# A two-layer diffusion backbone in f32 on one core: the last feed-forward with rstd behind the first product and the second product by token rows

## The chip, the cores and the metric

One core of a Trainium2 chip runs the whole program in one launch. The metric is the device time of one execution in microseconds, as the median of several runs; smaller is better. All inputs, weights and the output are float32 in device memory.

## The reference

A stream `x` of 256 latent tokens and a stream of 256 context tokens, both of width D = 1024, go through two layers. Each layer is a feed-forward, a token mixer and another feed-forward. Layer 0 mixes by latent attention, layer 1 by windowed attention. The last feed-forward and the final norm exist for the latent stream alone. What matters here, cut to the second feed-forward of the last layer and the end:

```python
def rms_norm(x, g):
    return x * lax.rsqrt(jnp.mean(x * x, axis=-1, keepdims=True) + EPS) * g

h = rms_norm(x, norm_g[layer, 2]) * (1.0 + mx[7]) + mx[6]     # modulate
g, u = jnp.split(h @ w_in, 2, axis=-1)                         # w_in 1024 x 5632
x = x + 0.5 * mx[8] * ((jax.nn.silu(g) * u) @ w_out)           # w_out 2816 x 1024
return rms_norm(x, final_norm_g)
```

`mx[c]` are nine vectors of 1,024 (shift, scale, gate for three sub-layers) from silu(c) @ mod_w + mod_b.

## The kernel before, in words

**Layout and products.** Features lie on the partitions: `xs[d]` holds features 128 d to 128 d + 127 of all tokens, latent ones in columns 0 to 255 (`X`), context ones in columns 256 to 511. A product runs in three f32r matmuls per block of 128 input features (`mm3`, lines 205 to 212): high half by high half, high by low, low by high. Activations and weights are split into such halves by `split` (lines 179 to 186): a cast on ACT makes the high half, a subtraction on DVE the low half. A matmul has a weight block of 128 x 128 as its stationary operand and tokens as columns: 512 where both streams go through, 256 for the latent stream alone.

**Weights** come as tiles of 512 KB through SP's DMA queue into a ring of three raw buffers and are split into rings of four high and four low buffers (`weight`, lines 188 to 203). PSUM has eight banks, all from one ring (`bank`, line 45).

**Sub-layers.** `Sublayer` (lines 249 to 338) prepares the normalized input of the next feed-forward or mixer while the sub-layer before ends. `closing` (lines 360 to 398) computes the last product of a sub-layer by output tiles of 128 features: `residual` (line 357, DVE) adds each to `xs[d]`, `grown` squares it (line 236, ACT) and sums the squares on POOL (line 242). Then `load_table` (line 247) loads ACT's table for the square root, `prefetch` loads the first two weights, and `stream` (line 279) makes rstd (`rstd_of`: column sums of the squares by a matmul with `ones`, line 221; root, line 223; reciprocal, line 225), scales every x by gain and rstd (lines 287, 288, 290) and splits it (lines 182, 183, 185, 186). Only then can `leading` (line 310) run the first two tiles of the next product.

**The last feed-forward** (`ffn`, lines 403 to 424, called on the last line of the program's body with `Final` as its follower): for each of 22 tiles of 128 of d_ff a gate and an up product of 24 matmuls each, SiLU (line 416), multiplication (line 418) and split. The tiles come in three groups of 8, 7 and 7; after each group `closing` multiplies the group by `w_out` and adds all 1,024 output features to `xs`. `Final` (lines 340 to 352) then makes rstd once more, scales, and writes eight transfers of 128 KB, features on partitions; the host transposes.

**Modulation vectors in the background.** `mod_in_background` (lines 142 to 161) computes one of the nine vectors by eight loads of 512 KB and eight accumulations on DVE (lines 149, 151), a sum over partitions on PE (line 157) and transposes (line 102). `pump` (line 169) issues a piece at a time between other work. The gate of the last feed-forward, vector 8 of layer 1, is made in the feed-forward ahead of the windowed attention.

**Order.** Every engine works its queue in order. A scheduler of the framework fixes that order when the program is built, from program order and a model of when each instruction is ready; `behind` (line 163) ties one instruction behind another by hand.

Of the kernel before, what the change touches and what calls it, by code (L numbers as in the profile page):

```python
# [10 lines left out]
F32 = mybir.dt.float32  # L11
# [3 lines left out]
ALU = mybir.AluOpType  # L15
# [22 lines left out]
def hybrid_backbone_kernel(ctx, tc, t, out):  # L38
# [298 lines left out]
                    mm3(o[:M, :w], self.terms(wt, M, slice(0, w)))  # L337
                    yield o

    class Final(Sublayer):  # L340


        def stream(self, s):
            r = self.rstd(s)
            for k in range(KT):
                y = strip()
                if k in POOL:
                    nc.gpsimd.tensor_tensor(y, xs[k][:, SL[s]], r, ALU.mult)
                    nc.scalar.activation(y, y, AF.Copy, scale=fng[:, k:k + 1])
                else:  # L350
                    nc.vector.scalar_tensor_tensor(y, xs[k][:, SL[s]], fng[:, k:k + 1], r, ALU.mult, ALU.mult)
                nc.sync.dma_start(out[k], y)

    def residual(l, chunk, d, o, streams):
        for s in streams:
            c = chunk * KT + d
# [46 lines left out]
    def ffn(sl, nxt, per_tile=0):  # L403
        l, which, streams = sl.l, sl.sub // 2, sl.streams
        w = T * len(streams)
        outs = sl.products(ffn_specs(l, which))
        done = sl.end
        for g, (f0, f1) in enumerate(GROUPS):
            gu = []
            for f in range(f0, f1):  # L410
                pump(per_tile // 2, done)
                og = next(outs)
                pump(per_tile - per_tile // 2, done)
                ou = next(outs)
                sg = tmp()
                nc.scalar.activation(sg[:, :w], og[:, :w], AF.Silu)  # L416
                pr = tmp()
                nc.vector.tensor_tensor(pr[:, :w], ou[:, :w], sg[:, :w], ALU.mult)  # L418
                hl = (r2k(), r2k())
                done = split(hl[0][:, :w], hl[1][:, :w], pr[:, :w])  # L420
                gu.append(hl)
            last = g == len(GROUPS) - 1
            closing([(t[f"wout{g}"][l, which, d], gu) for d in range(KT)], 2 + 6 * which, l, streams,
                    nxt if last else None, 2 if last else 0, per_tile // 2)


# [377 lines left out]
        closing([(t["swo"][d], O) for d in range(KT)], 5, l, (0,), nxt, 0)  # L804


    def load_tmp(name, n):
        s = r2k(n).bitcast(F32)
        nc.sync.dma_start(s, t[name])
        return s  # L810
# [47 lines left out]
    for k in range(1, KT + 1):  # L858
# [4 lines left out]
            inputs(k)  # L863
        if k in (1, 3, 5):
            lead_weight(sl.hi)
    fng = load_const("fng", (P, KT))
    qng = load_const("qng", (P, 4))
    kvng = load_const("kvng", (P, 2))
    ropeC = load_const("ropeC", (P, T))
# [24 lines left out]
    sl, nxt = nxt, Sublayer(1, 0, (0, 1), ffn_specs(1, 0)[:4])  # L894
    ffn(sl, nxt, 2)
    pump(1000)
    background.extend(mod_in_background(1, c, (0,)) for c in range(5, 9))
    sl, nxt = nxt, Sublayer(1, 1, (0, 1), [(t["swq"][m], 1024) for m in range(2)], (0,))
    ffn(sl, nxt, 2)
    pump(1000)  # L900
    sl, nxt = nxt, Sublayer(1, 2, (0,), ffn_specs(1, 1)[:2])
    swa(sl, nxt)
    ffn(nxt, Final(1, 3, (0,), ()))

def _layout(x, c, ctx, c_ctx, mod_w, mod_b, norm_g, final_norm_g, ffn_w_in, ffn_w_out, mla_w_down, mla_q_norm,
            mla_kv_norm, mla_w_uq, mla_w_ukv, mla_w_o, swa_w_qkv, swa_sink, swa_w_o, **unused):
    a = {}

    def put(name, v):
        a[name] = np.ascontiguousarray(v)

    def cols(v, n):
        return v.reshape(v.shape[:-1] + (n, P))

    def tiles(w, m):

        k, n = w.shape
        return w.reshape(k // P, P, n // m, m).transpose(2, 1, 0, 3)  # L920

    put("xT", np.concatenate([x[0].T, ctx[0].T], axis=1).reshape(KT, P, TT))
    put("cond", np.stack([c[0], c_ctx], axis=-1).reshape(KT, P, 2).transpose(1, 0, 2))
    put("modb", cols(mod_b, 72).transpose(2, 0, 1))
    put("ng", cols(norm_g, KT).transpose(3, 0, 1, 2))
    put("fng", cols(final_norm_g, KT).T)
    put("qng", cols(mla_q_norm[0], 4).T)
    put("kvng", cols(mla_kv_norm[0], 2).T)
    put("modo", mod_w[0][:, :2048].reshape(2, 4, P, 2, KT, P).transpose(4, 3, 0, 2, 1, 5).reshape(KT, 2, 2, P, 512))
    put("modw", mod_w.reshape(2, KT, P, 9, 1024).transpose(0, 3, 1, 2, 4))  # L930
    put("win", ffn_w_in.reshape(2, 2, KT, P, 2, NF, P).transpose(0, 1, 5, 4, 3, 2, 6).reshape(2, 2, NF, 2, P, 1024))
    wo = ffn_w_out.reshape(2, 2, NF, P, KT, P)
    for g, (f0, f1) in enumerate(GROUPS):
        put(f"wout{g}", wo[:, :, f0:f1].transpose(0, 1, 4, 3, 2, 5).reshape(2, 2, KT, P, (f1 - f0) * P))
    put("wdown", tiles(mla_w_down[0][:, :768], P).reshape(6, P, 1024))
    put("wkr", tiles(mla_w_down[0][:, 768:], 64).reshape(P, 512))
    uq = mla_w_uq[0].reshape(4, P, MLA_H, 192)
    put("wqn", uq[..., :128].reshape(4, P, 4, 2, P).transpose(2, 1, 3, 0, 4).reshape(4, P, 1024))
    put("wqr", uq[..., 128:].reshape(4, P, 2, 2, P).transpose(2, 1, 3, 0, 4).reshape(2, P, 1024))
    ukv = mla_w_ukv[0].reshape(2, P, MLA_H, 256)  # L940
    put("wkn", ukv[..., :128].reshape(2, P, 2, 4, P).transpose(2, 1, 3, 0, 4).reshape(2, P, 1024))
    put("wv", ukv[..., 128:].reshape(2, P, 2, 512).transpose(2, 1, 0, 3).reshape(2, P, 1024))
    put("mwo", tiles(mla_w_o[0], P).reshape(KT, P, 1024))
    put("swq", tiles(swa_w_qkv[0][:, :1024], P).reshape(8, P, 1024))
    put("swk", tiles(swa_w_qkv[0][:, 1024:1280], P).reshape(2, P, 1024))
    put("swv", swa_w_qkv[0][:, 1280:].reshape(2, 4, P, 256).transpose(0, 2, 1, 3).reshape(2, P, 1024))
    put("swo", tiles(swa_w_o[0], P).reshape(KT, P, 1024))
    put("sink", np.broadcast_to(swa_sink[0][None, :], (P, 16)))

    pos = np.arange(T)  # L950
    inv = np.exp(np.float32(-math.log(10000.0)) * np.arange(16, dtype=np.float32) / np.float32(16)).astype(np.float32)
    ang = np.concatenate([(pos // 64).astype(np.float32)[:, None] * inv, (pos % 64).astype(np.float32)[:, None] * inv], axis=-1)
    cos, sin = np.cos(ang).T.astype(np.float32), np.sin(ang).T.astype(np.float32)
    put("ropeC", np.concatenate([cos, cos, cos, cos]))
    put("ropeS", np.concatenate([-sin, sin, -sin, sin]))
    swap = np.zeros((P, 3, P), np.float32)
    row = np.arange(P)
    swap[row, 0, row ^ 32] = 1.0
    for half in range(2):
        swap[row, 1 + half, row % 64 ^ 32 | 64 * half] = 1.0  # L960
    put("perm", swap.reshape(P, 3 * P))
    put("ident", np.eye(P, dtype=np.float32))
    i, j = np.arange(P)[:, None], np.arange(P)[None, :]
    far = np.stack([np.where(j > i, NEG, 0.0), np.where(j < i, NEG, 0.0)], axis=1)
    put("band", far.astype(np.float32).reshape(P, 2 * P))
    return a
# [16 lines left out]
```

## Time and profile before

| | |
|---|---|
| median of 3 runs | 1747.94 us (1747.8 to 1748.0) |
| the profiled execution | 1748.32 us, of it 1746.3 us span from first to last instruction |
| PE / DVE / ACT / POOL busy | 1688.0 / 1088.4 / 669.7 / 187.6 us |
| mean granted TensorE clock | 0.989 of full speed |
| read from device memory | 240.11 MB, 138 GB/s over the span |

Times in the rows below are microseconds from the start of the span. A matmul's recorded time is longer than its slot, since matmuls overlap: the distance between two starts tells what one costs. PEld is the weight load, which runs beside the matmul before it.

### The profile page before, as it was taken

The numbers are of one execution on the slowest core, as the hardware profiler recorded it, in microseconds if no ns is written. First come the engines' busy times: TensorE is split into PE (matmuls) and PEld (weight loads), VectorE is DVE, ScalarE is ACT, GpSimd is POOL, SyncE is SP. The second block draws the span as 40 slices with busy tenths as digits, with TensorE's granted clock in tenths as the row PEclk, the third lists the DMA queues.
The fourth block names the chain that finished last, engine by engine and source line by source line (L and its number), as shares of the span: only waits on it lengthen the run. The fifth ranks groups of instructions, "written<-read, shape, count | busy, mean of one in ns | idle before, by whom it ended". The sixth has DMA issues, their size and how long they took to land.

```text
span 1746.3 us, 23850 instructions
## 1 busy us (share of the span) xinstructions
PE 1688.0 (97%) x9428; PEld 1439.0 (82%) x9428; DVE 1088.4 (62%) x1592; ACT 669.7 (38%) x1121; POOL 187.6 (11%) x183
## 2 busy tenths in 40 slices
PE   7999999999999999999999999999999989989997
PEld 4688888888788898888888888888888888889997
DVE  4877576646767467856946474645433679755554
ACT  4422222234556353222222342222222577554443
POOL 1000000004132130000000220000000452110001
PEclk9999999999999999999999999999999999999999
DMA  9556355431212126644735245634322221145552
GB/s 339 173 199 192 129 192 180 157 121 55 85 49 73 49 84 201 206 145 156 219 126 170 93 143 183 216 114 158 103 97 86 89 84 51 55 145 181 173 191 96
DMA packets 72831, 242.71 MB, mean 139 GB/s; under 512 B 8848, under 2 KB 10640, under 8 KB 72720
## 3 DMA queue, kind: packets, MB, share of 16 engines
q1 hardware_dynamic: 72720, 241.20, 41.9%
q8 instruction: 74, 1.21, 0.3%
q14 instruction: 37, 0.30, 0.1%
HBM read 240.11 MB, written 1.05 MB: 138 GB/s over the span
## 4 chain that ended last, share of the span: by engine, by line
PE 55%; DVE 4%; ACT 2%; issue 1%; POOL 1%; DMA 0%; POOLq 0%; ACTq 0%; DVEq 0%
PE bank L210 18%; PE bank L211 18%; PE bank L212 18%; DVE small L444 1%; DVE r2k L183 1%; PE bank L157 1%; DVE wlo L183 0%; DVE strip L225 0%; POOL r2k L183 0%; ACT r2k L182 0%; POOL r2k L287 0%; DVE small L457 0%; PE bank L102 0%; ACT whi L182 0%; DVE x L464 0%
## 5 line engine op out<-in xcount | busy, mean ns | idle before, releaser
L210 PE MATMUL bank<-r2k,whi 128*128 128x512 f32 (+1 forms) x2610 | 918.4, 353 | 9.3 <-ACT r2k L185 4.7
L211 PE MATMUL bank<-r2k,whi 128*128 128x512 f32 (+1 forms) x2610 | 915.3, 351 | 9.8 <-POOL r2k L183 6.1
L212 PE MATMUL bank<-r2k,wlo 128*128 128x512 f32 (+1 forms) x2610 | 912.2, 350 | 4.1 <-POOL wlo L183 2.2
L182 ACT CAST whi<-wraw 128x1024 fp32r<-128x1024 f32 (+1 forms) x313 | 321.7, 1028 | 886.8 <-PE bank L211 527.8
L210 PEld LDWEIGHTS bank<-r2k,whi 128*128 128x128 f32 x2610 | 494.6, 190 | 89.9 <-ACT whi L182 9.2
L211 PEld LDWEIGHTS bank<-r2k,whi 128*128 128x128 f32 x2610 | 496.2, 190 | 78.8 <-POOL r2k L183 8.6
L212 PEld LDWEIGHTS bank<-r2k,wlo 128*128 128x128 f32 x2610 | 495.7, 190 | 69.4 <-POOL wlo L183 3.0
L183 DVE TENSOR_TENSOR wlo<-wraw,whi 128x1024 fp32r<-128x1024 f32 (+1 forms) x302 | 362.9, 1204 | 134.7 <-ACT whi L182 124.7
L151 DVE SCALAR_TENSOR_TENSOR big<-modraw,conds,big 128x1024 f32<-128x1024 f32 x196 | 242.2, 1279 | 13.9 <-DMA modraw<-in_modw 13.3
L357 DVE SCALAR_TENSOR_TENSOR x<-bank,mod,x 128x256 f32<-128x256 f32 x192 | 85.7, 478 | 179.9 <-PE bank L212 179.9
L242 POOL TENSOR_TENSOR strip<-strip 128x256 f32<-128x256 f32 x64 | 65.2, 1032 | 1137.1 <-ACT strip L236 1110.4
L418 DVE TENSOR_TENSOR tmp<-bank,tmp 128x512 f32<-128x512 f32 (+1 forms) x88 | 54.9, 624 | 179.6 <-PE bank L212 177.7
L183 DVE TENSOR_TENSOR r2k<-bank,r2k 128x512 fp32r<-128x512 f32 (+2 forms) x107 | 62.0, 616 | 18.2 <-ACT r2k L182 17.9
L182 ACT CAST r2k<-bank 128x512 fp32r<-128x512 f32 (+2 forms) x107 | 52.4, 541 | 16.4 <-PE bank L212 15.7
L183 DVE TENSOR_TENSOR r2k<-tmp,r2k 128x512 fp32r<-128x512 f32 (+1 forms) x88 | 54.4, 618 | 1.5 <-ACT r2k L182 1.4
L182 ACT CAST r2k<-tmp 128x512 fp32r<-128x512 f32 (+1 forms) x88 | 49.7, 566 | 9.9 <-DVE tmp L418 9.5
L416 ACT ACTIVATE tmp<-bank 128x512 f32<-128x512 f32 (+1 forms) x88 | 47.3, 538 | 6.8 <-PE bank L212 6.8
L444 DVE TENSOR_REDUCE small<-bank 128x1 f32<-128x512 f32 (+1 forms) x64 | 37.7, 614 | 0.3 <-PE bank L645 0.2
L236 ACT ACTIVATE strip<-x 128x256 f32<-128x256 f32 x80 | 30.5, 410 | 17.9 <-DVE x L357 17.0
L225 DVE RECIPROCAL strip<-strip 128x256 f32<-128x256 f32 x14 | 24.5, 1750 | 19.9 <-ACT strip L223 19.9
L186 DVE SCALAR_TENSOR_TENSOR r2k<-r2k,mod 128x256 fp32r<-128x256 f32 x45 | 30.3, 696 | 8.7 <-ACT r2k L185 8.5
L450 ACT ACTIVATE tmp<-bank,small 128x512 f32<-128x512 f32 x32 | 21.9, 688 | 18.4 <-DVE small L446 12.3
(152 smaller groups left out, 1067.1 us busy)
## 6 DMA issues: line engine op xcount, KB each, us to landing
wraw<-in_win SPq DMA_DIRECT2D x172, 512.0 KB, 3.5
modraw<-in_modw SPq DMA_DIRECT2D x128, 512.0 KB, 4.2
wraw<-in_wout SPq DMA_DIRECT2D x64, 448.0 KB, 3.3
wraw<-in_wout SPq DMA_DIRECT2D x32, 512.0 KB, 3.5
r2k<-in_modo SPq DMA_DIRECT2D x32, 256.0 KB, 5.7
wraw<-in_mwo SPq DMA_DIRECT2D x8, 512.0 KB, 3.5
wraw<-in_swq SPq DMA_DIRECT2D x8, 512.0 KB, 3.5
wraw<-in_swo SPq DMA_DIRECT2D x8, 512.0 KB, 3.4
```

The source lines that it names most:

```text
L151: nc.vector.scalar_tensor_tensor(acc[s], raw, conds[:, kt, s:s + 1], acc[s], ALU.mult, ALU.add)
L182: nc.scalar.copy(hi, src)
L183: return engine.tensor_tensor(lo, src, hi.bitcast(F32), ALU.subtract)
L210: nc.tensor.matmul(o, lhsT=ah, rhs=bh, start=(i == 0), stop=False)
L211: nc.tensor.matmul(o, lhsT=ah, rhs=bl, start=False, stop=False)
L212: nc.tensor.matmul(o, lhsT=al, rhs=bh, start=False, stop=(i == n - 1))
L236: nc.scalar.activation(q, x, AF.Square)
L242: nc.gpsimd.tensor_tensor(self.parts[0], self.parts[0], q, ALU.add)
L357: nc.vector.scalar_tensor_tensor(xs[d][:, SL[s]], o[:, SL[s]], mod[l][:, s, c:c + 1], xs[d][:, SL[s]], ALU.mult, ALU.add)
L416: nc.scalar.activation(sg[:, :w], og[:, :w], AF.Silu)
L418: nc.vector.tensor_tensor(pr[:, :w], ou[:, :w], sg[:, :w], ALU.mult)
L444: nc.vector.tensor_reduce(top[:, j:j + 1], o[:, :w], axis=AX.X, op=ALU.max)
```

## The change

The last feed-forward gets a function of its own, `last_ffn`, and an input class `Raw` in place of a normalized input.

- `Raw.grown` splits gain times x, without rstd, as soon as each x is complete, and appends the shift vector as two more columns (258 in all). `Raw.stream` makes rstd alone. The first product's result is multiplied by rstd when it leaves the bank, and the shift's column is added (as the bias of SiLU for the gate, as an addend for up).
- The second product takes the activations as the stationary operand, 128 tokens at a time, and `w_out` rows as 512 columns. Four banks (two blocks of tokens, two halves of features) sum over all 22 tiles. The product of tile f - 1 is issued after the first product of tile f.
- The gate is made as a row that is the same on all partitions (`mod_row_in_background`), now during the last feed-forward; `xs` is transposed by PE at tiles 5, 7, 9 and 11.
- The final norm works on rows of tokens; four transfers of 256 KB write the output, two from SP's queue and two from ACT's. The host no longer transposes.

```diff
-    class Final(Sublayer):
-
-
-        def stream(self, s):
-            r = self.rstd(s)
-            for k in range(KT):
-                y = strip()
-                if k in POOL:
-                    nc.gpsimd.tensor_tensor(y, xs[k][:, SL[s]], r, ALU.mult)
-                    nc.scalar.activation(y, y, AF.Copy, scale=fng[:, k:k + 1])
-                else:
-                    nc.vector.scalar_tensor_tensor(y, xs[k][:, SL[s]], fng[:, k:k + 1], r, ALU.mult, ALU.mult)
-                nc.sync.dma_start(out[k], y)
...
+    class Raw(Sublayer):
+
+        W = T + 2
+
+        def grown(self, s, d):
+            x = xs[d][:, X]
+            zh, zl = r2k(self.W), r2k(self.W)
+            nc.scalar.activation(zh[:, :T], x, AF.Identity, scale=self.gain(0, d))
+            nc.vector.scalar_tensor_tensor(zl[:, :T], x, self.gain(0, d), zh[:, :T].bitcast(F32), ALU.mult, ALU.subtract)
+            shift = self.shift(0, d).to_broadcast([P, 2])
+            nc.scalar.copy(zh[:, T:], shift)
+            nc.gpsimd.tensor_tensor(zl[:, T:], shift, zh[:, T:].bitcast(F32), ALU.subtract)
+            self.hs.append((zh, zl))
+            self.squares[s].add(x)
+
+        def terms(self, w, M, cols=None):
+            return [(pair(w, slice(None), slice(k * M, (k + 1) * M)), self.hs[k]) for k in range(KT)]
+
+        def stream(self, s):
+            self.r = self.rstd(s)
+            return self.r[:, 0:1]
+
+        def leading(self, s):
+            for k in range(KT):
+                for wt, o, M in self.lead:
+                    mm3(o[:M, :self.W], self.terms(wt, M), (k,))
+
+        def products(self, specs):
+            for i, (ap, size) in enumerate(specs):
+                if i < len(self.lead):
+                    yield self.lead[i][1]
+                else:
+                    wt = weight(ap, size)
+                    o = bank()
+                    mm3(o[:, :self.W], self.terms(wt, P))
+                    yield o
+
+    def mod_row_in_background(row, c):
+
+        acc = big().bitcast(F32)[:, :1024]
+        for kt in range(KT):
+            raw = ring.tile([P, 1024], F32, tag="modraw", name="modraw", bufs=2)
+            nc.sync.dma_start(raw, t["modw"][1, c, kt])
+            if kt == 0:
+                nc.vector.tensor_scalar_mul(acc, raw, conds[:, kt, 0:1])
+            else:
+                nc.vector.scalar_tensor_tensor(acc, raw, conds[:, kt, 0:1], acc, ALU.mult, ALU.add)
+            yield
+        for half in range(2):
+            cols = slice(half * 512, half * 512 + 512)
+            b = bank()
+            nc.tensor.matmul(b, lhsT=ones, rhs=acc[:, cols], start=True, stop=True)
+            nc.vector.tensor_tensor(row[:, cols], b, row[:, cols], ALU.add)
+            yield
+
+    def last_ffn(sl):
+
+        gate, fngr = (big().bitcast(F32)[:, :1024] for _ in range(2))
+        nc.sync.dma_start(gate, t["gater"])
+        nc.sync.dma_start(fngr, t["fngr"])
+        background.append(mod_row_in_background(gate, 8))
+        outs = sl.products(ffn_specs(1, 1))
+        acc = [[bank() for _ in range(2)] for _ in range(2)]
+        xt = [[None] * 2 for _ in range(2)]
+        r = sl.r
+        done = None
+
+        def second(f, gu, w):
+            for i in range(2):
+                rows = slice(i * P, (i + 1) * P)
+                for h in range(2):
+                    cols = slice(h * 512, h * 512 + 512)
+                    for j, (a, b) in enumerate(((0, 0), (0, 1), (1, 0))):
+                        nc.tensor.matmul(acc[i][h], lhsT=gu[a][:, rows], rhs=w[b][:, cols],
+                                         start=(f == 0 and j == 0), stop=(f == NF - 1 and j == 2))
+
+        held = None
+        for f in range(NF):
+            pump(1, done)
+            og, ou = next(outs), next(outs)
+            wt = weight(t["woutn"][f])
+            if held:
+                second(f - 1, *held)
+            ends = small(2)
+            nc.scalar.copy(ends[:, 0:1], og[:, T:T + 1])
+            nc.scalar.copy(ends[:, 1:2], ou[:, T:T + 1])
+            g, u = tmp(T), tmp(T)
+            nc.vector.tensor_tensor(g, og[:, X], r, ALU.mult)
+            nc.scalar.activation(g, g, AF.Silu, bias=ends[:, 0:1])
+            nc.vector.tensor_tensor(u, ou[:, X], r, ALU.mult)
+            nc.vector.scalar_tensor_tensor(u, u, ends[:, 1:2], g, ALU.add, ALU.mult)
+            gu = (r2k(T), r2k(T))
+            hi = nc.scalar.copy(gu[0], u)
+            done = nc.vector.tensor_tensor(gu[1], u, gu[0].bitcast(F32), ALU.subtract)
+            held = gu, wt
+            if f in (5, 7, 9, 11):
+                i, h = (f - 5) // 4, (f - 5) // 2 % 2
+                b = bank()
+                for d in range(4):
+                    nc.tensor.transpose(b[:, d * P:(d + 1) * P], xs[4 * h + d][:, i * P:(i + 1) * P], ident)
+                xt[i][h] = r2k().bitcast(F32)
+                nc.scalar.copy(xt[i][h], b)
+        pump(1000)
+        with behind(hi):
+            nc.scalar.activation(small(1), r[:, 0:1], AF.Sqrt)
+        second(NF - 1, *held)
+        for i in range(2):
+            sums, rs = small(2), small(1)
+            scaled = []
+            for h in range(2):
+                cols = slice(h * 512, h * 512 + 512)
+                x = xt[i][h]
+                y = tmp()
+                nc.vector.scalar_tensor_tensor(y, acc[i][h], 0.5, gate[:, cols], ALU.mult, ALU.mult)
+                nc.vector.tensor_tensor(x, x, y, ALU.add)
+                nc.scalar.activation(y, x, AF.Square, accum_out=sums[:, h:h + 1])
+                nc.gpsimd.tensor_tensor(x, x, fngr[:, cols], ALU.mult)
+            nc.vector.tensor_tensor(rs, sums[:, 0:1], sums[:, 1:2], ALU.add)
+            nc.scalar.activation(rs, rs, AF.Sqrt, scale=1.0 / D, bias=eps)
+            nc.vector.reciprocal(rs, rs)
+            nc.vector.tensor_scalar_mul(xt[i][0], xt[i][0], rs)
+            nc.sync.dma_start(out[i, :, :512], xt[i][0])
+            nc.scalar.activation(xt[i][1], xt[i][1], AF.Copy, scale=rs)
+            nc.scalar.dma_start(out[i, :, 512:], xt[i][1])
+
+
...
-    fng = load_const("fng", (P, KT))
...
-    background.extend(mod_in_background(1, c, (0,)) for c in range(5, 9))
+    background.extend(mod_in_background(1, c, (0,)) for c in range(5, 8))
...
-    sl, nxt = nxt, Sublayer(1, 2, (0,), ffn_specs(1, 1)[:2])
+    sl, nxt = nxt, Raw(1, 2, (0,), ffn_specs(1, 1)[:2])
     swa(sl, nxt)
-    ffn(nxt, Final(1, 3, (0,), ()))
+    last_ffn(nxt)
...
+    put("fngr", np.broadcast_to(final_norm_g[None, :], (P, D)))
+    put("gater", np.broadcast_to(mod_b[1, None, 8 * D:], (P, D)))
+    put("woutn", ffn_w_out[1, 1].reshape(NF, P, D))
...
-    out = nc.dram_tensor("out_x", (KT, P, T), F32, kind="ExternalOutput").ap()
+    out = nc.dram_tensor("out_x", (2, P, D), F32, kind="ExternalOutput").ap()
```

## Rows read from the trace of the kernel before

**Rows 1.** The page: busy time of the engines, bytes moved per slice.

```profile
PE 1688.0 (97%) x9428; PEld 1439.0 (82%) x9428; DVE 1088.4 (62%) x1592; ACT 669.7 (38%) x1121; POOL 187.6 (11%) x183
...
GB/s 339 173 199 192 129 192 180 157 121 55 85 49 73 49 84 201 206 145 156 219 126 170 93 143 183 216 114 158 103 97 86 89 84 51 55 145 181 173 191 96
```

**Rows 2.** Windows: stretch, length, busy of PE, PEld, DVE, ACT, POOL, clock, DMA, GB/s.

```profile
1310.00:1370.00 60.00, 60.00 (x270) 49.83 (x270) 21.87 (x31) 18.16 (x29) 7.97 (x8) 1.00 0.31 97
1655.00:1715.00 60.00, 59.98 (x500) 59.92 (x500) 34.33 (x44) 26.34 (x36) 0.00 (x0) 1.00 0.57 183
```

**Rows 3.** Timeline, start of the last feed-forward: start, duration, engine, instruction, idle before.

```profile
1533.17 0.28 PE L212 MATMUL bank<-r2k,wlo 128*128 128x256 f32 x1
...
1533.49 0.70 PE L221 MATMUL bank<-strip,ones 128*128 128x256 f32 x2
1533.49 0.48 DVE L357 SCALAR_TENSOR_TENSOR x<-bank,mod,x 128x256 f32<-128x256 f32 x1 [0.65 <-PE bank L212]
1534.37 0.41 ACT L236 ACTIVATE strip<-x 128x256 f32<-128x256 f32 x1
...
1536.69 1.75 DVE L225 RECIPROCAL strip<-strip 128x256 f32<-128x256 f32 x1 [0.97 <-ACT strip L223]
...
1539.56 0.80 PE L210 MATMUL bank<-r2k,whi 128*128 128x256 f32 x2 [4.03 <-ACT r2k L185]
```

**Rows 4.** Windows, the same start; columns as in rows 2.

```profile
1536.00:1540.00 4.00, 0.44 (x2) 0.44 (x2) 3.28 (x4) 1.29 (x5) 0.96 (x1) 0.61 0.38 131
1540.00:1544.00 4.00, 4.00 (x20) 3.78 (x20) 3.46 (x7) 2.96 (x7) 1.77 (x2) 0.53 0.00 0
```

**Rows 5.** Timeline of PE: sums and transposes of one modulation vector, transposes in attention.

```profile
1224.44 1.05 PE L157 MATMUL bank<-big,ones 128*32 128x512 f32 x4
...
1230.42 0.46 PE L102 MATMUL bank<-c_ident,tmp 64*128 64x64 f32 x4
...
1506.16 1.25 PE L472 MATMUL bank<-c_ident,tmp 128*128 128x128 f32 x10
```

**Rows 6.** Timeline of ACT, early in the last feed-forward.

```profile
1550.91 1.04 ACT L182 CAST whi<-wraw 128x1024 fp32r<-128x1024 f32 x1
1551.85 0.41 ACT L182 CAST r2k<-tmp 128x256 fp32r<-128x256 f32 x1
```

**Rows 7.** Groups by line and form, 1300 us to the end: busy, mean ns, idle before.

```profile
L183 DVE TENSOR_TENSOR wlo<-wraw,whi 128x1024 fp32r<-128x1024 f32 x71 | 88.2, 1243 | 54.7 <-ACT whi L182 54.4
L182 ACT CAST whi<-wraw 128x1024 fp32r<-128x1024 f32 x76 | 79.7, 1049 | 110.2 <-PE bank L211 56.0 <-issue 54.2
...
L450 ACT ACTIVATE tmp<-bank,small 128x512 f32<-128x512 f32 x16 | 11.0, 691 | 1.3 <-DVE small L448 1.2
...
L462 ACT ACTIVATE tmp<-tmp,small 128x512 f32<-128x512 f32 x8 | 5.8, 723 | 1.9 <-DVE small L459 1.8
...
L418 DVE TENSOR_TENSOR tmp<-bank,tmp 128x512 f32<-128x512 f32 x4 | 2.8, 692 | 14.0 <-PE bank L212 14.0
L183 DVE TENSOR_TENSOR r2k<-tmp,r2k 128x512 fp32r<-128x512 f32 x4 | 2.7, 685 | 0.0
```

**Rows 8.** Timeline, the tail: PE's last product and the last scaling.

```profile
1733.58 0.28 PE L212 MATMUL bank<-r2k,wlo 128*128 128x256 f32 x1
...
1743.17 0.51 ACT L349 ACTIVATE strip<-strip,c_fng 128x256 f32<-128x256 f32 x1 [2.34 <-POOL strip L348]
```

**Rows 9.** Timeline of DVE and POOL near the end of the second product.

```profile
1724.72 1.09 DVE L183 TENSOR_TENSOR wlo<-wraw,whi 128x896 fp32r<-128x896 f32 x1 [0.41 <-ACT whi L182]
...
1725.14 1.26 POOL L242 TENSOR_TENSOR strip<-strip 128x256 f32<-128x256 f32 x1 [1.26 <-ACT strip L236]
...
1727.42 0.74 POOL L242 TENSOR_TENSOR strip<-strip 128x256 f32<-128x256 f32 x1 [1.01 <-ACT strip L236]
```

**Rows 10.** The output's tile: its DMA issues (min/median/max ns) and landing.

```profile
L352 SPq DMA_DIRECT2D out_x<-strip x8: 333/402/456, 1739.7 to 1743.7; - x8
...
DMA to landing us min/median/max: 1.7/1.8/1.9
```

More of the change, by code (lines that the diff above doesn't have):

```diff
@@ L422, in ffn @@
             last = g == len(GROUPS) - 1
-            closing([(t[f"wout{g}"][l, which, d], gu) for d in range(KT)], 2 + 6 * which, l, streams,
+            closing([(t[f"wout{g}"][2 * l + which, d], gu) for d in range(KT)], 2 + 6 * which, l, streams,
                     nxt if last else None, 2 if last else 0, per_tile // 2)
@@ L925, in _layout @@
     put("ng", cols(norm_g, KT).transpose(3, 0, 1, 2))
-    put("fng", cols(final_norm_g, KT).T)
+    put("fngr", np.broadcast_to(final_norm_g[None, :], (P, D)))
+    put("gater", np.broadcast_to(mod_b[1, None, 8 * D:], (P, D)))
+    put("woutn", ffn_w_out[1, 1].reshape(NF, P, D))
     put("qng", cols(mla_q_norm[0], 4).T)
@@ L931, in _layout @@
     put("win", ffn_w_in.reshape(2, 2, KT, P, 2, NF, P).transpose(0, 1, 5, 4, 3, 2, 6).reshape(2, 2, NF, 2, P, 1024))
-    wo = ffn_w_out.reshape(2, 2, NF, P, KT, P)
+    wo = ffn_w_out.reshape(4, NF, P, KT, P)[:3]
     for g, (f0, f1) in enumerate(GROUPS):
-        put(f"wout{g}", wo[:, :, f0:f1].transpose(0, 1, 4, 3, 2, 5).reshape(2, 2, KT, P, (f1 - f0) * P))
+        put(f"wout{g}", wo[:, f0:f1].transpose(0, 3, 2, 1, 4).reshape(3, KT, P, (f1 - f0) * P))
     put("wdown", tiles(mla_w_down[0][:, :768], P).reshape(6, P, 1024))
@@ L981 @@
     got = r.results[0]["out_x"]
-    return np.ascontiguousarray(got.reshape(D, T).T[None])
+    return np.ascontiguousarray(got.reshape(1, T, D))
```

## The prediction

> **What bounds the kernel now.** I began with the page: TensorE (PE) is busy for 97% of the span, VectorE (DVE) for 62%, ScalarE (ACT) for 38% [rows 1]. So first I look for time in which PE does not stream, then for PE work that gets cheaper.
>
> The windows by stage give two prices of a matmul in a full stream. With 256 columns, in the last feed-forward, 500 took 60.00 us: 0.120 us each, with weight loads busy throughout. With 512 columns, in the feed-forward with both streams, 270 took 60.00 us: 0.222 us each, with loads busy 83% of the time [rows 2]. A column costs less in the wide form: two of 256 are 0.240, one of 512 is 0.222.
>
> The timeline at the start of the last feed-forward shows the one big hole. The last product of attention issues at 1533.17 and its slot ends at 1533.29. PE then does the column sums of the squares (two pairs of 0.70 us), waits for square, table load, root and reciprocal, and starts the first product only at 1539.56, after a recorded wait of 4.03 us [rows 3]. Over that idle time the granted clock falls to 0.61 and then 0.53, the lower of its two levels, so the matmuls of 1540 to 1544 run slow as well (20 in 4 us) [rows 4]. From 1533.29 to the end of the last slot of the second product at 1733.70 [rows 3, 8] are 200.4 us. The 1,584 matmuls (1,056 of the first product, 528 of the second) need 190.1 at 0.120. The remaining 10.3 are 1.4 for the column sums and **8.9 us of stall and slow clock**. Behind 1733.70 stands a **tail of 12.6 us**: residual, square, table, root, reciprocal, scaling, eight output transfers; the last scaling starts at 1743.17 [rows 8].
>
> **The change part by part.**
>
> Start. The products no longer wait for rstd: high and low halves of gain times x are made as each x leaves the bank, and rstd multiplies the result. The two first weights are there already, as before. Of the 48 leading matmuls 42 belong to k = 0 to 6 and cover 5.1 us. For k = 7, x is ready at 1533.97 [rows 3]; its high half is an ACT instruction of 256 columns (0.41 by the square), its low half a DVE one (0.48 by the residual) that may stand behind one weight low half of 1.24 [rows 3, 7]: ready by 1536.2, covered until 1538.4. The last square follows high half and the two-column copy on ACT, so it ends about 0.8 later than at present, near 1535.6. If PE keeps the column sums ahead of the leading products it waits about 1.3 us for it; if not, nothing. I take 0.6. From square end to reciprocal end are 3.7 us now (1534.78 to 1538.44) [rows 3], so rstd comes near 1539.3. PE is with the leading products until about 1540.5, and has two more banks and 48 more matmuls (5.8 us) before an eviction matters: covered. Gain 8.9 - 0.6 = **-8.3**. In the loop that closes attention each weight takes 24 matmuls, 2.88 us; DVE there gets 0.48 more on top of 1.24 and 0.48, ACT about 0.8 on top of 1.05 and 0.41: below 2.88 both, at nothing; uncovered, 7 times what exceeds.
>
> First product: 258 columns. Between the two prices, (0.222 - 0.120)/256 = 0.0004 us a column: +0.0008 x 1,056 = **+0.9**. Bounds: no change, and the 512 price (+108), if columns were charged in blocks; I take the line.
>
> Second product: 528 x 0.120 = 63.4 against 264 x 0.222 = 58.7: **-4.7**. The page "TensorE: Matmul & The Clock Gate" of the Trainium skill, section "Back-to-back issue gap", gives N/2.4 + 2.5 ns for a single matmul's gap: by it my estimate is 57.6 against 57.0, a gain of 0.7 in place of 4.7. The trace disagrees: the two row prices are 11 and 6 ns above it.
>
> Transposes of x, 16 of 128x128: ten in a row took 1.25 [rows 5], so **+2.0**. Their copies are four ACT instructions of 512, with no PE work waiting.
>
> The gate as a row: eight DMAs of 512 KB and eight DVE accumulations go from the feed-forward before attention to this one. There they lay beside full PE streaming and free nothing. PE loses four passes (1.05) and four transposes (0.46) there [rows 5]: **-1.5**. Here come two f32 matmuls of 512 columns against full `ones`: the column sums (two passes of 256 in 0.70) make it 2.8, the strips' 1.05 is the lower bound; **+2.8** by the nearer shape.
>
> DMA and queues: three weights of 512 KB per tile of d_ff are the same bytes as now, at 183 GB/s [rows 2]; one of modw for eight tiles adds 0.52 MB per 8.5 us, 62 GB/s; 245 is below the 339 of the page's first slice [rows 1]. Gate and final gain are two more, at the start. On SP's queue the next weights stand behind each modw load, which waits for DVE to release its buffer; three raw buffers, a whole tile of 8.5 us, cover that. At nothing; uncovered, up to one accumulation (about 1.24) per tile for eight, 10.
>
> DVE per tile: 3 x 1.24, four instructions of 256 at up to 0.48, one accumulation of 1.24: 6.9 of 8.47 us (48 x 0.1208 + 12 x 0.222). ACT: 3 x 1.05 and four of at most 0.41: 4.8. Both fit. The low-half matmuls of the last tile need a chain from its up product (copy, SiLU, DVE, cast, DVE, some 2.3 us) under the 2.7 us of the previous tile's second product. For filling and emptying I allow **+1.0**, bounds 0 and 5.
>
> Tail. First bank ready 9 x 0.222 - 0.16 = 1.9 us before the end of PE's slots, the last 0.16 after it. DVE does four gate multiplications (0.75: 0.69 for a bank of 512, and as the residual adds to 256) and four adds (0.69) in a row [rows 7], plus sum, reciprocal and one scaling of the first half (1.1): last add at about 5.0. Square and its accumulator read 0.9, POOL multiplication 1.5 (twice 0.74), ACT scaling 0.72 [rows 7, 9], hops 0.3: 8.4. From the start of the last scaling to the end are 3.1 now, 2.6 behind it [rows 8]: 11.0. But POOL beside a DVE instruction with two SBUF inputs took 1.26, not 0.74 [rows 9]; with 2.5 each for the first two POOL works, the four end at 8.5 and the tail is 12.0. No row shows DVE waiting for POOL; if the second half's adds also stood behind one POOL multiplication of 1.5, the tail would be 13.5. The page "SBUF — State Buffer" of the Trainium skill, section "Who interferes with whom", has such a wait on both sides: the later of a DVE instruction with two SBUF inputs and a POOL instruction that reads SBUF blocks until the earlier is done. The trace agrees for POOL's side, which ended 0.59 us behind DVE. The output's halves: a landing took 1.8 for 128 KB, and 256 KB adds about 0.4 at 339 GB/s; two of four go by ACT's queue, which no row shows; SP's issue took 0.40 [rows 10], and behind the first one on ACT stand the second half's squares. Bounds 9.5 and 13.5; I take 11.5: **-1.1**.
>
> Sum: -8.3 + 0.9 - 4.7 + 2.0 - 1.5 + 2.8 + 1.0 - 1.1 = **-8.9 us**. The profiled execution took 1748.32 (span 1746.3 and 2.0 around it); the median of the runs is 0.4 lower, 1747.94. Forecast: 1748.32 - 8.9 - 0.4 = **1739.0**.
>
> **The rivals.**
>
> (a) Slower: the next weight is queued behind the eviction. Four buffers hold split weights, and the second product's weight holds one for a whole tile more. The next gate weight gets its buffer when a gate product ends (T); PE needs it 24 x 0.121 + 12 x 0.222 = 5.6 later. Made at once it is ready at T + 2.4. If ACT's order puts its cast behind copy, SiLU and cast of the current tile, which cannot end before T + 4.7, it is ready at T + 7.0: 1.4 late, 21 times, +29, 1768. It decides from 0.42 us a tile on. For it: ACT and DVE are strictly in order, and DVE goes from 57% [rows 2] to 81%. Against it: now the weight cast stands before the cast of the activation in ACT's order (1550.91 against 1551.85) [rows 6].
>
> (b) The start keeps half its hole: column sums and the term of k = 7 stay ahead on PE, or rstd is late at the first eviction. +4 to +5, 1743.5: faster by little or no change. For it: the order of PE now; against it: 42 matmuls that need neither.
>
> (c) DVE and POOL wait for each other in the tail, 13.5 instead of 11.5: 1741. POOL's part is in a row, DVE's is unseen. (This is the rule of the page on SBUF.)
>
> (d) The small prices are all at their lower bounds (gate row 1.05, transposes hidden in waits, start without a wait, tail 9.5): 1739.0 - 1.75 - 1.0 - 0.6 - 2.0 = 1733.6.
>
> (e) Columns in blocks: 258 like 384 or 512, +54 or more. Nothing in the rows speaks for it except that no width between occurs.
>
> (f) The wide form gains little in the second product, 0.7 instead of 4.7: 1743. Both prices are from long full streams, which speaks against it. (This is what the gap of the page on TensorE would give.)
>
> **How the numbers follow.** Forecast 0.44, (a) 0.11, (b) 0.12, (c) 0.12, (d) 0.17, (e) 0.02, (f) 0.02. The range reaches from (d) with a little more to the upper end of (b): 1732.5 to 1746. A measurement here tells about 0.2%, 3.5 us, from no change: faster needs 1744.4. Forecast, (c), (d), (f) and nearly half of (b) lie below it: 0.80. The rest of (b): 0.07. (a) and (e): 0.13.
>
> **What would show it.** Right: after the last attention product PE idles below 2 us and the granted clock stays at 1.0 through the start; the first product's matmuls 0.121 apart, the second's 0.222; no PE wait on weights in the last feed-forward; the tail 11 to 12 us, its end on POOL's multiplication and the scaling. Wrong: ACT weight casts behind casts of activations and PE waiting for them once per tile (a); a clock below 1.0 at the start (b); POOL or DVE above 1.5 in the tail (c); matmuls of 258 columns at 0.17 or more (e).

## The result, and the profile after

| | before | changed |
|---|---|---|
| median | 1747.97 us | 1736.92 us (1735.05 to 1737.44, 4 runs) |
| ratio, 95% interval | | 0.9939 [0.9926, 0.9951] |
| profiled execution | 1748.32 us, span 1746.3 | 1735.05 us, span 1733.0 |

Eleven microseconds less, where 8.9 were forecast. The profiled execution of the changed kernel is the quickest of its four and gains 13.3; where the other two come from is told below. The page of the changed kernel answers to [rows 1]; the third line is the chain of work that ended last, share of the span by engine:

```profile
span 1733.0 us, 23362 instructions
...
PE 1678.4 (97%) x9172; PEld 1421.7 (82%) x9172; DVE 1099.6 (63%) x1615; ACT 676.5 (39%) x1171; POOL 180.5 (10%) x180
...
PE 85%; DVE 6%; issue 3%; ACT 2%; POOL 1%; DMA 1%; SPq 0%; POOLq 0%; ACTq 0%; DVEq 0%
```

The busy shares barely moved. What changed is where PE is not busy. This is the timeline at the start of the last feed-forward, which answers to [rows 3]:

```profile
1528.96 0.28 PE L212 MATMUL bank<-r2k,wlo 128*128 128x256 f32 x1
1529.28 0.70 PE L221 MATMUL bank<-strip,ones 128*128 128x256 f32 x2
1529.63 0.47 PE L210 MATMUL bank<-r2k,whi 128*128 128x258 f32 x1
...
1530.57 0.40 ACT L236 ACTIVATE strip<-x 128x256 f32<-128x256 f32 x1
...
1531.14 0.59 PE L221 MATMUL bank<-strip,ones 128*128 128x256 f32 x2
...
1532.89 1.75 DVE L225 RECIPROCAL strip<-strip 128x256 f32<-128x256 f32 x1 [0.98 <-ACT strip L223]
...
1541.84 0.40 PE L866 MATMUL bank<-whi,r2k 128*128 128x512 f32 x1
```

The last attention product's slot ends at 1529.08 and the first product's first matmul starts at 1529.63; before, those were 6.3 us apart. The second pair of column sums slips in between two products, as soon as the last square is done. PE did not wait for it. And the clock stays up, in the windows that answer to [rows 4], with the same columns:

```profile
1536.00:1540.00 4.00, 4.00 (x35) 4.00 (x34) 3.16 (x5) 3.97 (x8) 0.00 (x0) 1.00 0.22 49
1540.00:1544.00 4.00, 4.00 (x27) 3.60 (x26) 3.87 (x7) 2.51 (x5) 0.00 (x0) 1.00 0.78 242
```

From there to the end of the second product the trace lists no wait of PE at all. The chain of work (start, duration, what) in the middle of it shows the tile of 8.50 us, and the two additions to it:

```profile
1559.03 2.75 PE bank L866 x12
1567.53 2.75 PE bank L866 x12
1576.03 2.75 PE bank L866 x12
1578.78 0.44 PE bank L892 x4
...
1596.66 0.86 PE bank L844 x2
```

A block of 12 wide matmuls takes 2.75 us, 0.229 each, and 48 of the first product take the other 5.75, 0.120 each. Four transposes (L892) take 0.44, one half of the gate row's sum (L844) 0.86.

The tail, timeline of the engines behind PE:

```profile
1719.10 1.37 DVE L906 SCALAR_TENSOR_TENSOR tmp<-bank,big 128x512 f32<-128x512 f32 x2 [1.39 <-PE bank L866]
...
1721.91 6.08 POOL L909 TENSOR_TENSOR r2k<-r2k,big 128x512 f32<-128x512 f32 x4 [192.35 <-ACT tmp L908]
...
1723.12 0.68 DVE L907 TENSOR_TENSOR r2k<-r2k,tmp 128x512 f32<-128x512 f32 x1
...
1723.79 1.68 DVE L907 TENSOR_TENSOR r2k<-r2k,tmp 128x512 f32<-128x512 f32 x1
...
1725.39 1.49 DVE L913 TENSOR_SCALAR r2k<-r2k,small 128x512 f32<-128x512 f32 x1
...
1726.80 1.21 DVE L910 TENSOR_TENSOR small<-small 128x1 f32<-128x1 f32 x1
...
1728.63 0.72 ACT L915 ACTIVATE r2k<-r2k,small 128x512 f32<-128x512 f32 x1 [0.29 <-DVE small L912]
```

DVE's first instruction starts when 15 of the last 24 wide matmuls are done, so PE's slots end 9 x 0.229 - 0.16 = 1.9 us later, at 1721.0, and the tail is 12.0 us (before: 12.6). While POOL works from 1721.91 to 1727.99, one DVE add takes 1.68 us where the one before it takes 0.68, a scaling takes 1.49, and a sum of one element per partition 1.21: it ends at 1728.01, when POOL is done. Taken one by one, POOL's four multiplications take 1.27, 1.79, 1.71 and 1.45 us and end at 1723.18, 1724.92, 1726.59 and 1727.99. DVE's add of 1.68 ends 0.55 behind the second of them, its scaling 0.29 behind the third, its sum of 1.21 with the fourth; POOL's later three are longer than its first. So each side stands still for the other.

**Where the time went, between the two traces.** The last attention product ends 4.2 us earlier (1529.08 against 1533.29 [rows 3]); from there to the end of PE's slots are 191.9 us instead of 200.4, so -8.5; the tail gives -0.6. Together 13.3. Of the 4.2 us ahead of the last feed-forward, 1.3 are there already at the first residual (135.05 against 136.32 us), before anything that was changed; over all ten profiles that residual starts anywhere from 134.81 to 136.78. About 1.0 each arises near 640 and near 1020 us, where the code is the same but the granted clock was not: its mean over 630 to 645 is 0.89 before and 1.00 after (0.89 again in the second profile of the changed kernel), over 1012 to 1040 0.94 and 1.00. About 1.9 arise between 1130 and 1230 us, where the gate's sums and transposes are gone. And 1.0 is given back in attention: the stretch between the residuals at 1371.70 and at 1513.33 takes 141.6 us before and 142.6 here, but 141.2 to 142.9 in the seven kernels below that differ from the changed kernel only behind it, so this is not the change's either. So some 2.3 of the 13.3 are a difference between executions, and 11.0 are the change's (8.5, 1.9 and 0.6), by that trace.

### The profile page after: what moved, and what is told of

The parts are those of the page before. It is cut to its first block, busy times and chain, and to the rows that moved or that the text cites. A ratio compares the mean times of both kernels' runs of the same rounds, so it can differ in the third digit from the quotient of the medians.

```text
span 1733.0 us, 23362 instructions
## 1 busy us (share of the span) xinstructions
PE 1678.4 (97%) x9172; PEld 1421.7 (82%) x9172; DVE 1099.6 (63%) x1615; ACT 676.5 (39%) x1171; POOL 180.5 (10%) x180
## 4 chain that ended last, share of the span: by engine, by line
PE 85%; DVE 6%; issue 3%; ACT 2%; POOL 1%; DMA 1%; SPq 0%; POOLq 0%; ACTq 0%; DVEq 0%
PE bank L210 26%; PE bank L211 26%; PE bank L212 26%; PE bank L866 3%; DVE small L430 1%; DVE r2k L183 1%; PE bank L157 1%; DMA r2k<-in_modo 1%; DVE r2k L290 1%; DVE strip L225 1%; PE bank L458 1%; DVE wlo L183 1%; PE bank L221 1%; POOL r2k L183 1%; POOL r2k L287 0%
## 5 line engine op out<-in xcount | busy, mean ns | idle before, releaser
L211 PE MATMUL bank<-r2k,whi 128*128 128x512 f32 (+2 forms) x2434 | 863.5, 355 | 10.1 <-POOL r2k L183 5.7
L210 PE MATMUL bank<-r2k,whi 128*128 128x512 f32 (+2 forms) x2434 | 867.1, 358 | 4.5 <-ACT r2k L182 2.1
L212 PE MATMUL bank<-r2k,wlo 128*128 128x512 f32 (+2 forms) x2434 | 860.8, 354 | 4.1 <-POOL wlo L183 2.2
L210 PEld LDWEIGHTS bank<-r2k,whi 128*128 128x128 f32 x2434 | 458.5, 189 | 84.8 <-ACT whi L182 8.4
L211 PEld LDWEIGHTS bank<-r2k,whi 128*128 128x128 f32 x2434 | 460.1, 189 | 79.3 <-POOL r2k L183 8.0
L212 PEld LDWEIGHTS bank<-r2k,wlo 128*128 128x128 f32 x2434 | 460.1, 189 | 69.3 <-POOL wlo L183 3.0
L404 DVE TENSOR_TENSOR tmp<-bank,tmp 128x512 f32<-128x512 f32 x66 | 45.5, 690 | 163.7 <-PE bank L212 162.7
L866 PE MATMUL bank<-whi,r2k 128*128 128x512 f32 x176 | 57.9, 391 | 0.0
L183 DVE TENSOR_TENSOR r2k<-tmp,r2k 128x512 fp32r<-128x512 f32 x66 | 45.1, 684 | 1.5 <-ACT r2k L182 1.4
L182 ACT CAST r2k<-tmp 128x512 fp32r<-128x512 f32 x66 | 41.0, 622 | 9.7 <-DVE tmp L404 9.2
L402 ACT ACTIVATE tmp<-bank 128x512 f32<-128x512 f32 x66 | 38.9, 589 | 6.7 <-PE bank L212 6.7
L866 PE MATMUL bank<-wlo,r2k 128*128 128x512 f32 x88 | 34.5, 392 | 0.0
```

Source lines behind the costliest of these rows:

```text
L182: nc.scalar.copy(hi, src)
L183: return engine.tensor_tensor(lo, src, hi.bitcast(F32), ALU.subtract)
L210: nc.tensor.matmul(o, lhsT=ah, rhs=bh, start=(i == 0), stop=False)
L211: nc.tensor.matmul(o, lhsT=ah, rhs=bl, start=False, stop=False)
L212: nc.tensor.matmul(o, lhsT=al, rhs=bh, start=False, stop=(i == n - 1))
L866: nc.tensor.matmul(acc[i][h], lhsT=gu[a][:, rows], rhs=w[b][:, cols], start=(f == 0 and j == 0), stop=(f == NF - 1 and j == 2))
```

## The experiments

Eight kernels ran in two groups, each group beside the kernel before on its own chip (medians there 1746.01 us for the first four of the table and 1746.51 for the last four). The ratio to the kernel before of the same group is what is compared.

| run | median us | ratio, 95% interval |
|---|---|---|
| normalized input first | 1743.79 | 0.9985 [0.9976, 0.9993] |
| rstd behind the product, alone | 1740.31 | 0.9962 [0.9948, 0.9976] |
| tail without POOL | 1734.90 | 0.9929 [0.9916, 0.9941] |
| tail reordered | 1734.91 | 0.9932 [0.9919, 0.9944] |
| the changed kernel again | 1736.55 | 0.9942 [0.9929, 0.9954] |
| gate of the bias alone | 1734.43 | 0.9933 [0.9921, 0.9946] |
| weight casts last | 1765.63 | 1.0111 [1.0097, 1.0125] |
| tail by hand | 1733.24 | 0.9925 [0.9912, 0.9939] |

### The start put back

```diff
-    sl, nxt = nxt, Raw(1, 2, (0,), ffn_specs(1, 1)[:2])
+    sl, nxt = nxt, Sublayer(1, 2, (0,), ffn_specs(1, 1)[:2])
...
-            nc.vector.tensor_tensor(g, og[:, X], r, ALU.mult)
-            nc.scalar.activation(g, g, AF.Silu, bias=ends[:, 0:1])
-            nc.vector.tensor_tensor(u, ou[:, X], r, ALU.mult)
-            nc.vector.scalar_tensor_tensor(u, u, ends[:, 1:2], g, ALU.add, ALU.mult)
+            nc.scalar.activation(g, og[:, X], AF.Silu)
+            nc.vector.tensor_tensor(u, ou[:, X], g, ALU.mult)
```

> Only the input of the last feed-forward goes back: it is normalized with rstd before the first product, as in the kernel before; the second product by token rows, the gate row and the norm by rows stay. Theory: the hole at the start (8.9 us of stall and slow clock) is what the change removed there, so it comes back whole: 1736.9 + 8.5 = about 1745.4 us, with PE idle some 6 us behind the last attention product and the granted clock at its lower level for some microseconds. Rival 1: the hole is not worth that, the gain is from the second product and from earlier stages: at most +3, 1740 or less. Rival 2: the lighter eviction (one DVE and one ACT instruction less per tile) gives something back: 1743 or less.

Measured: 0.9985, that is 2.6 us below the kernel before, where the theory's 1745.4 against 1747.97 is 0.9985 too. Against the changed kernel's 0.9942 the edit costs 0.0043, some 7.5 us. Its timeline and its windows over the start (columns as in [rows 2]) are those of the kernel before over again:

```profile
1535.30 0.79 PE L210 MATMUL bank<-r2k,whi 128*128 128x256 f32 x2 [4.03 <-ACT r2k L185]
```

```profile
1532.00:1536.00 4.00, 0.70 (x2) 0.50 (x2) 3.50 (x4) 1.30 (x4) 0.96 (x1) 0.60 0.36 131
1536.00:1540.00 4.00, 4.00 (x21) 3.98 (x21) 3.24 (x6) 2.96 (x8) 1.77 (x2) 0.55 0.00 0
```

The wait of 4.03 us is the same to the hundredth, and the clock falls to 0.60 and 0.55. Rival 1 falls: the start carries the greater part of the gain. For rival 2 nothing speaks: PE waits for no eviction in either kernel, so a lighter one has nothing to give back.

### The start alone

The class `Raw` comes into the kernel before as it stands in the change; the other lines are these, cut:

```diff
+                if isinstance(sl, Raw):
+                    ends = small(2)
...
+                    nc.vector.tensor_tensor(sg[:, X], og[:, X], sl.r, ALU.mult)
+                    nc.scalar.activation(sg[:, X], sg[:, X], AF.Silu, bias=ends[:, 0:1])
...
-    sl, nxt = nxt, Sublayer(1, 2, (0,), ffn_specs(1, 1)[:2])
+    sl, nxt = nxt, Raw(1, 2, (0,), ffn_specs(1, 1)[:2])
     swa(sl, nxt)
     ffn(nxt, Final(1, 3, (0,), ()))
```

> The kernel before with one part of the change alone: rstd behind the first product; the second product in three groups by output features, the gate in columns and the norm by columns stay. Theory: the start's 8.5 us and nothing else, about 1739.4 us. Rival: the second product and the row norm carry the gain, and this part alone gives 3 us or less: 1745 or more.

Measured: 0.9962, 6.6 us below the kernel before, with an interval of 4.2 to 9.1; the theory's 0.9951 lies within it, the rival's 0.998 does not. Timeline of PE at the start and at the end of its second product:

```profile
1532.78 0.28 PE L212 MATMUL bank<-r2k,wlo 128*128 128x256 f32 x1
1533.10 0.70 PE L221 MATMUL bank<-strip,ones 128*128 128x256 f32 x2
1533.44 0.47 PE L210 MATMUL bank<-r2k,whi 128*128 128x258 f32 x1
...
1725.62 0.28 PE L212 MATMUL bank<-r2k,wlo 128*128 128x256 f32 x1
```

From 1532.90 to 1725.74 are 192.8 us, 7.6 less than before. In this kernel the 258 columns show: 336 matmuls in an unbroken row took 40.60 us, 0.1208 each, and 1,056 times the 0.0008 above 0.120 are 0.9: without them the gain in this trace would be 8.5. The two halves of the change, 2.6 (all but the start) and 6.6 (the start), add up to 9.2 of its 10 to 11 us.

### The tail, in three steps

First the POOL multiplications go:

```diff
-                nc.gpsimd.tensor_tensor(x, x, fngr[:, cols], ALU.mult)
...
-            nc.vector.tensor_scalar_mul(xt[i][0], xt[i][0], rs)
-            nc.sync.dma_start(out[i, :, :512], xt[i][0])
-            nc.scalar.activation(xt[i][1], xt[i][1], AF.Copy, scale=rs)
-            nc.scalar.dma_start(out[i, :, 512:], xt[i][1])
+            for h in range(2):
+                cols = slice(h * 512, h * 512 + 512)
+                nc.vector.scalar_tensor_tensor(xt[i][h], xt[i][h], rs, fngr[:, cols], ALU.mult, ALU.mult)
+                (nc.scalar if h else nc.sync).dma_start(out[i, :, cols], xt[i][h])
```

> The changed kernel with the final gain multiplied by DVE together with rstd (one instruction per half), no POOL work in the tail. Theory: POOL and DVE waited for each other there (an add took 1.68 us, a sum of one column 1.21); without POOL every DVE add takes 0.7, the sum 0.4 or less, and although DVE has more to do the tail falls from 12.0 to about 11.0: 1736 us. Rival: DVE's queue is the bound anyway and four instructions of 0.7 more make up for what POOL held: tail 12 or more.

Then the last two tiles' second products are interleaved, and both halves' residuals come ahead of the scalings:

```diff
...
+        second(NF - 1, *held, ((0, 0), (0, 1)))
+        second(NF - 2, *before_last, ((1, 1),))
+        second(NF - 1, *held, ((1, 0), (1, 1)))
...
```

> As the kernel without POOL in the tail, and the last two tiles of the second product are ordered so that the first 128 tokens are complete nine matmuls before the end, with both halves' residuals ahead of either half's scaling on DVE. Theory: DVE's chain starts 0.7 us earlier against the end of PE and does not wait for the second half's squares: tail about 10.3, 1735.3 us. Rival: the last transfer and its end (3.6 us behind the last scaling) and DVE's sixteen instructions set the tail whatever their order: as without the reordering.

Measured: 0.9929 and 0.9932, by ratios 0.0013 and 0.0010 (2.3 and 1.7 us) below the changed kernel's 0.9942, with intervals that overlap its own. The traces are sharper. PE's slots end 0.23 us behind the last start of a matmul, and the tail is what follows:

| | last start | span | tail |
|---|---|---|---|
| changed kernel, second profile | 1722.26 | 1734.5 | 12.0 |
| without POOL | 1722.88 | 1733.3 | 10.2 |
| reordered | 1723.04 | 1733.9 | 10.6 |
| by hand | 1720.27 | 1729.3 | 8.8 |

Timeline of DVE without POOL:

```profile
1725.69 0.68 DVE L907 TENSOR_TENSOR r2k<-r2k,tmp 128x512 f32<-128x512 f32 x1
...
1726.28 1.41 DVE L914 SCALAR_TENSOR_TENSOR r2k<-r2k,small,big 128x512 f32<-128x512 f32 x2
...
1727.61 0.15 DVE L909 TENSOR_TENSOR small<-small 128x1 f32<-128x1 f32 x1
```

The add that took 1.68 takes 0.68, and the sum that took 1.21 takes 0.15, with no other edit to them: they had stood still for POOL. The reordering alone gave nothing, as its rival had it. DVE started 0.7 us earlier against the end of PE, and then stood idle for two roots: the first stood behind the second half's squares on ACT, and the sum that the second root needs stood behind the first half's scalings on DVE:

```profile
1726.70 0.16 DVE L916 RECIPROCAL small<-small 128x1 f32<-128x1 f32 x1 [0.92 <-ACT small L915]
...
1729.10 0.16 DVE L916 RECIPROCAL small<-small 128x1 f32<-128x1 f32 x1 [0.72 <-ACT small L915]
```

So in the last step the order of the small instructions is tied by hand (`behind`):

```diff
...
+        q = root(0, ins[1])[1]
+        added(1, 0, ys[0], q)
+        a = added(1, 1, ys[1], q)
...
+        first = scaled(0, 0)
+        total1, _ = root(1, first)
+        second_half = scaled(0, 1, total1)
```

> As the kernel with the reordered tail, and the order of the small instructions written out: the first half's sum and root ahead of the second half's squares on ACT, the second half's sum between the first half's two scalings on DVE. In the kernel with the reordered tail DVE stood idle 0.92 us for the first root behind the squares, 0.72 for the second. Theory: DVE's queue is the tail now, both waits go, and the tail is 10.6 - 1.6 = about 9.0 us: 3 us less than the changed kernel. Rival: transfers and the end behind the last scaling (3.2 us) or new waits for squares hold it at 10 or more.

Measured: 0.9925, 3.3 us less than the changed kernel in the same group (1733.24 against 1736.55), tail 8.8. Timeline of DVE:

```profile
1722.93 0.16 DVE L937 RECIPROCAL small<-small 128x1 f32<-128x1 f32 x1
...
1723.12 0.75 DVE L925 SCALAR_TENSOR_TENSOR r2k<-r2k,small,big 128x512 f32<-128x512 f32 x1
...
1723.81 0.16 DVE L918 TENSOR_TENSOR small<-small 128x1 f32<-128x1 f32 x1
1723.89 0.74 DVE L925 SCALAR_TENSOR_TENSOR r2k<-r2k,small,big 128x512 f32<-128x512 f32 x1
...
1724.74 1.42 DVE L925 SCALAR_TENSOR_TENSOR r2k<-r2k,small,big 128x512 f32<-128x512 f32 x2
```

Both waits are gone, and the trace lists no wait of DVE from the first bank to the last scaling. This kernel leaves nothing out and has the lowest ratio of all that ran. Its interval still overlaps the changed kernel's, [0.9912, 0.9939] and [0.9929, 0.9954]; that the tail is what shrank is in the trace.

### The changed kernel again, and without the gate's computation

> The changed kernel once more, beside the others of this group on the same chip, so that they are compared with it and not only with the kernel before: ratio to before near 0.994.

Measured: 0.9942, as before. In the second kernel the background work is taken out:

```diff
-        background.append(mod_row_in_background(gate, 8))
```

> The changed kernel without the gate row's computation: the gate is taken as its bias alone, so eight loads of modw, eight DVE accumulations and two f32 matmuls of 512 columns with their two additions are left out. Theory: all of it but the two matmuls is hidden; they stood 0.86 us each on PE in the changed kernel's chain, so 1.7 us less than the changed kernel, and PE's tiles stay 8.5 us long. Rival: the loads in front of the weights on SP's queue, or DVE's extra 1.24 us per tile, cost more than PE shows: 4 us or more less, in the first eight tiles.

Measured: 2.1 us less by medians (1734.43 against 1736.55) and 1.6 by ratios, with intervals that overlap; 1.7 expected, and 4 or more by the rival. The windows over the first tiles, the changed kernel and then this one:

```profile
1545.00:1605.00 60.00, 60.00 (x426) 56.14 (x424) 43.66 (x57) 29.57 (x52) 0.00 (x0) 1.00 0.68 229
```

```profile
1545.00:1605.00 60.00, 60.00 (x428) 56.54 (x427) 37.01 (x52) 29.41 (x52) 0.00 (x0) 1.00 0.58 187
```

DVE falls from 73% to 62% and the transfers from 229 to 187 GB/s, and PE is busy for all of the 60 us in both, in tiles of 8.50. In the changed kernel's chain, by the starts of the blocks of wide matmuls, only the two tiles that hold the f32 matmuls are longer for the gate row, by 0.9 each. So loads and accumulations are hidden, as the prediction had it, and the two f32 matmuls are what the gate row costs.

### The rival that ended slower, made true

```diff
...
-                    wt = weight(ap, size)
+                    wt = weight(ap, size, after=self.cast)
...
-            hi = nc.scalar.copy(gu[0], u)
+            hi = sl.cast = nc.scalar.copy(gu[0], u)
```

> The changed kernel with one order forced on ACT: the casts of the next two first-product weights stand behind the cast of the current tile's activation, which is the place in program order; the scheduler had put them ahead. Theory (rival a of the prediction, made true): the gate weight is ready 7.0 us after its buffer came free where PE needs it 5.6 after, 1.4 us late in each of about 20 tiles: +29 us, about 1766, with PE waiting on ACT or DVE for a weight once per tile. Rival: the fourth buffer and the weight of the second product that is made a tile ahead take this up, PE waits less than 0.3 us a tile: +6 us or less.

Measured: 1765.63, 29.1 us slower than the changed kernel in the same group and 1.1% slower than the kernel before. The price came out, but not at the place. The waits of PE's matmuls over the last feed-forward (total us, times, longest):

```profile
PE bank L867 <- ACT r2k L886: 15.0, 18, 1.4
PE bank L210 <- ACT whi L182: 4.0, 1, 4.0
```

PE waits 18 times for the cast of the *activation* (L886), once for a weight. With its weights late, the scheduler had arranged PE's order anew: in the trace part of the second product runs right behind the first product of its own tile, and the tile of delay that covers the eviction is gone. Timeline of PE in one such tile, from the end of the first product (L212) on:

```profile
1660.76 0.29 PE L212 MATMUL bank<-r2k,wlo 128*128 128x258 f32 x1
1660.88 0.40 PE L867 MATMUL bank<-whi,r2k 128*128 128x512 f32 x1
...
1662.71 0.51 PE L867 MATMUL bank<-whi,r2k 128*128 128x512 f32 x1 [0.96 <-ACT r2k L886]
```

From this block's first start to the next block's are 9.55 us, where a tile of the changed kernel has 8.50. At the start of the feed-forward stands the wait of 4.0 for a weight, and over 1540 to 1548 the granted clock is 0.57. So a single bound order on ACT turns this group's gain of 10 us into a loss of 19; that the sum of 1.4 us times 21 fits this other mechanism is in part chance.

## Why the prediction was right, point by point

**The start** (-8.3): right in its mechanism, and exact in part by luck. Counted by starts in PE's timeline, what the start takes beyond its matmuls falls from 9.5 to 1.2 us, column sums included: -8.3. PE lost nothing where 0.6 was allowed, since the column sums did not stay ahead of the products. But the hole of 8.9 was read too large. It held all that PE lost up to the end of the second product, and 0.9 of that lies at the three changes from the first to the second product, 0.3 at each. There PE waits for the low half of the last tile, here in its timeline in the kernel before:

```profile
1591.38 0.28 PE L210 MATMUL bank<-r2k,whi 128*128 128x256 f32 x1
1591.69 0.39 PE L211 MATMUL bank<-r2k,whi 128*128 128x256 f32 x1
1591.91 0.28 PE L212 MATMUL bank<-r2k,wlo 128*128 128x256 f32 x1
```

The starts are 0.30 and 0.22 apart instead of 0.12. With the groups these changes are gone too, a gain that the prediction had put down to the start. Putting the start back and doing it alone give 7.5 and 6.6 us by ratios, and 7.6 by the second one's trace, in which the columns cost 0.9. That the lower clock was part of the hole shows in the kernel with the start put back.

**First product** (+0.9): 0.0008 for the two columns is what the unbroken row measured. In the changed kernel, where 48 first-product matmuls alternate with 12 wide ones, they cost 0.120 like 256 columns; the kernel with 256 columns in the same alternation has the same 5.75 us a block. So the term is near nothing there; why the alternation hides the two columns is not shown. Rival (e) falls.

**Second product** (-4.7): the term that was mis-sized most. Per tile 8.50 us stand against 72 x 0.120 = 8.64, which over 22 tiles is 3.1 for both products, where -3.8 was forecast. The second product alone is 264 x 0.229 = 60.5 in place of 58.7: -2.9. The price of 0.222 was 60 us divided by 270 instructions [rows 2], and nine of these have 256 columns. The 260 wide ones of that window, in a row from 1310.05 to 1368.76, start 0.2267 apart, and a block of twelve in the changed kernel shows 0.229. By the rule for a single matmul's gap in the Trainium skill's page "TensorE: Matmul & The Clock Gate", section "Back-to-back issue gap", the estimate for 512 columns is 0.216: the trace does not agree, by 13 ns.

**Transposes** (+2.0): 4 x 0.44 = 1.8. **Gate row** (+2.8): 2 x 0.86 = 1.7, between the two bounds. The 0.70 that it was priced from is the recorded time of two overlapping passes, longer than their slots; here a pass of 512 columns takes 0.43. **Gate in the earlier stage** (-1.5): about 1.9 by the residuals' starts. **Filling and emptying** (+1.0): nothing, PE shows no wait.

**Tail** (-1.1): 12.0 where 11.5 was forecast and 12 to 13.5 stood as the range with waits on both sides. Rival (c) was the mechanism, at about a quarter of its price above the forecast. The working had 12.0 too, but for waits of POOL alone. The Trainium skill's page "SBUF — State Buffer", section "Who interferes with whom", has a DVE instruction with two SBUF inputs and a POOL instruction that reads SBUF block each other, the later one until the earlier is done. The trace agrees: DVE's add took 1.68 beside POOL's work and 0.68 without.

Rivals (a) and (b) did not happen. Made true by hand, (a) cost what it was priced at, but by another path. The median of 1736.92 lies between the forecast and (d): several small terms lay at their cheap ends. The sum of the terms as measured in the changed kernel's trace (-8.5 over PE's part with all additions, -0.6 in the tail, -1.9 in the earlier stage) is -11.0, beside -11.0 by the medians of the result and -10.0 by those of the group in which the changed kernel ran again.

## What to carry to other kernels

A normalization need not stand ahead of a product: scale the rows of the result, feed the shift in as more columns, and the reduction, table load and reciprocal hide behind matmuls that do not need them. Price matmul forms from an unbroken block of the same form in the timeline, not from a window's count. In a short tail, where nothing is hidden, keep POOL off SBUF while DVE adds, and order the small sums and roots by hand.

## What the runs showed of the hardware that was not expected

In unbroken rows at full granted clock the matmuls start 0.1200, 0.1208 and 0.2267 us apart at 256, 258 and 512 columns. These three lie on one line: 1/2.4 ns for a column and 13.3 ns for a matmul.

A DVE sum of one column per partition took 1.21 us beside POOL's multiplication and 0.15 without it: how long an instruction stands still there does not follow from its size. A `TENSOR_SCALAR`, with one SBUF tile as input, took 1.49 in the changed kernel's first half, under POOL's work, and 0.48 in its second, after it.

The granted clock differs between executions in stages whose code is the same: two places, near 640 and 1020 us, cost about 1 us each in the profile of the kernel before and nothing in that of the changed kernel, whose second profile has the first of them again (0.89 over 630 to 645, where the first profile has 1.00). One profile of each kernel can so mislead by 2 us where the whole effect is 11.
